# A gather of tokens for the experts, rebuilt with float32r one-hot slots and dealt out over the down products, with eight expert tiles loaded ahead

## The chip, the cores and the metric

One core of a Trainium2 chip runs the whole layer. The metric is device microseconds (us) for one execution. TensorE (PE) does the matrix products, VectorE (DVE), ScalarE (ACT) and GpSimd (POOL) the elementwise work, and DMA transfers are issued from the queues of SyncE (SP) and ACT.

## The reference, cut to what matters

The layer has two token mixers, a merge, an output projection and then a mixture of experts in which each of 16 experts chooses 64 of the 512 latent tokens. The part that the change touches is the expert stage:

```python
def expert_choice_ffn(h, router_w, w_gate, w_up, w_down):
    cap = max(1, (CAPACITY_FACTOR * n) // N_EXPERTS)          # 64
    aff = jax.nn.softmax(jnp.einsum('bnd,de->bne', h, router_w).astype(jnp.float32), axis=-1)
    gate, idx = lax.top_k(jnp.swapaxes(aff, 1, 2), cap)
    xs = jax.vmap(lambda hb, ib: hb[ib])(h, idx)              # the gather: 64 tokens of 2048 for each expert
    a = jnp.einsum('becd,edf->becf', xs, w_gate)
    u = jnp.einsum('becd,edf->becf', xs, w_up)
    y = jnp.einsum('becf,efd->becd', jax.nn.silu(a) * u, w_down) * gate[..., None].astype(h.dtype)
    ...                                                       # scatter-add back to the 512 tokens
```

Here h = modulate(rms_norm(x_lat)). The weights are float32: per expert 2048x1024 twice and 1024x2048 once, 24 MB, so 384 MB for the stage.

## The kernel before, in words

The program runs in this order: the input projections with the HGRN2 branch, then the gated DeltaNet branch, then `branches` (it reads the mixers' results, `yraw`, back on the ACT queue and splits them into a high and a low float32r part), `merge` (two branch products `pb0`, `pb1` for each of 16 blocks of channels), `project` (the output projection `po` and the router's logits `lg`), `prefetch` (which issues the first expert tiles), `route` (the top 64 of each expert) and `experts`.

Weights of the dense stages go through `split`: a 512 KB tile `wraw` (three buffers) is loaded on SP, ACT makes `whi` (two buffers), DVE makes `wlo`, and three products follow for each tile of weights. In `project` a step of 2 contraction blocks needs one `wraw` and feeds 24 products of 512 columns.

The experts are taken in pairs, two experts' 64 tokens making up the 128 rows. Each pair takes 48 tiles `ew` of 1 MB through `take()`: 32 of the gate and up weights, then 16 of the down weights. `pair(...)` takes two of them (one for each expert) and issues 8 products. `pgt`/`put` (tiles `pg`, `pu`) collect gate and up, `pys` (tiles `py`, `pu`) the down product. `prefetch` hands out the tiles: the first 18 (numbered 0 to 17 here) are issued ahead, 11 (`EW`) into the buffers `ew`, then 7 into `aa`, `row5`, four `xo` and `xs`, which are not used again for weights. From tile 18 on, tile n takes the buffer of the tile 11 before it in the ring of `ew`, once PE has used that one. Four of the 11 buffers (`ew1`) exist already while `project` runs, the other seven (`ew2`) only after it.

The gather before is one-hot: `begin` makes on DVE `oh`, a 128x64 one-hot tile for each of 4 token blocks and 2 experts, scaled by `rstd`, and on POOL `og`, the same scaled by the router's weight. `gather(pr, kc)` multiplies four blocks of channels of `x1` by it in plain float32 (16 products of 128 columns), and ACT applies the modulation to give `xs`. Two of a pair's four quarters run while the silu of the pair before is made, two after the products of k = 2 and k = 6 of the pair itself. After the last gate product `og` is transposed into `sct` and summed into `gs`. `scatter` puts the results back with `tokens`, dealt out by `step()` over the next pair's products.

PE's order in `branches` and in `experts` is the order of the code (a manual schedule); in `merge` and `project`, and on the other engines everywhere, a scheduler chooses it from a simulated timeline and from which memory is free. Each DMA also waits for the one that used its completion semaphore before; there are eight of these, dealt round over both queues.

Of the kernel before, what the change touches and what calls it, by code (L numbers as in the profile page):

```python
# [8 lines left out]
F32 = mybir.dt.float32  # L9
# [8 lines left out]
D = 2048  # L18
# [24 lines left out]
class Kern:  # L43
# [27 lines left out]
        return ap[:, k // 2 * 256 + k % 2:k // 2 * 256 + 256:2]  # L71

    pe = 0.0
    EW = 11
    pool_split = False

    def mm(self, out, lhsT, rhs, start=True, stop=True):
# [954 lines left out]
    def project(self):  # L1032
# [9 lines left out]
        self.bcol = self.fcol[:, 0]  # L1042
        V.tensor_scalar(self.acol, self.fcol[:, 1], 1.0, None, op0=OP.add)
        V.tensor_tensor(self.acol, self.acol, self.nffn, op=OP.mult)
        self.ew1 = self.pool("ew1", bufs=self.opt.get("e1", 4))
        sp = self.pool("pj")
        row2 = sp.tile([128, D], F32, name="row2")
        nc.scalar.dma_start(row2, self.row_d[0])
# [72 lines left out]
        self.close("pj")  # L1121
        self.close("m")
        self.close("w")
        self.ew2 = self.pool("ew2", bufs=self.EW - self.opt.get("e1", 4), side="right")

    def prefetch(self):

        nc, I = self.nc, self.I
        sp = self.ex = self.pool("ex")
        wg = I["w_gate"][0].rearrange("e (k p i) n -> e p k (i n)", p=128, i=2)  # L1130
        wu = I["w_up"][0].rearrange("e (k p i) n -> e p k (i n)", p=128, i=2)
        wd = I["w_down"][0].rearrange("e (k p) n -> e p k n", p=128)
        big = self.big = lambda: sp.tile([128, D], F32, name="xo", bufs=4)
        nld = [0]

        def load(t):
            src, pair = t
            n = nld[0]
            nld[0] += 1
            m = n - self.EW  # L1140
            if m in (0, 1):
                w = sp.tile([128, D], F32, name=("aa", "row5")[m])
            elif 2 <= m < 6:
                w = big()
            elif m == 6:
                w = sp.tile([128, D], F32, name="xs", bufs=2)
            else:
                if m > 6:
                    n -= 7
                w = (self.ew1 if n % self.EW < self.opt.get("e1", 4) else self.ew2).tile([128, D], F32, name="ew")  # L1150
            k, n = src.shape[1:]
            w = w[:, :k * n].rearrange("p (k n) -> p k n", k=k)
            nc.sync.dma_start(w, src)
            return w.rearrange("p k (i n) -> p (k i) n", i=2) if pair else w

        tiles = []
        for pr in range(E // 2):
            es = (2 * pr, 2 * pr + 1)
            for k in range(KT // 2):
                for w in (wg, wu):  # L1160
                    tiles += [(w[e][:, k:k + 1], True) for e in es]
            for ns in self.blocks(pr):
                n = self.rows(ns)
                for f in range(0, 8, n):
                    tiles += [(wd[e][:, f:f + n, ns], False) for e in es]
        ahead = [load(t) for t in tiles[:self.EW + 7]]
        rest = iter(tiles[self.EW + 7:])
        self.take = lambda: ahead.pop(0) if ahead else load(next(rest))

    def route(self):  # L1170
# [4 lines left out]
        xp = self.xp  # L1175
        self.slot = xp.tile([128, 4, 16], F32, name="slot")
        sp = self.ex
        t64 = lambda name, n: sp.tile([128, NL], F32, name=name, bufs=n)[:64, :256]
        pp = self.pool("rop", space=PSUM)
        A, wk, gt, eq, on, cs = (t64(n, b) for n, b in (("y", 2), ("y", 2), ("sct", 1), ("og", 1), ("oh", 2), ("oh", 2)))  # L1180
# [6 lines left out]
        m = xp.tile([64, 2, 64], F32, name="m64")  # L1187
        for i in range(8):
            src = wk if i else pa
            m8 = m[:, 0, i * 8:i * 8 + 8]  # L1190
# [44 lines left out]
    def experts(self):  # L1235
# [7 lines left out]

        def begin(pr):

            oh = sp.tile([128, 4, 2, 64], F32, name="oh", bufs=2)
            og = sp.tile([128, 4, 2, 64], F32, name="og", bufs=1)
            for t in range(4):
                for e in range(2):
                    n = 2 * pr + e  # L1250
                    V.tensor_scalar(oh[:, t, e], self.iota64, self.slot[:, t, n:n + 1], self.rstd[:, t:t + 1],
                                    op0=OP.is_equal, op1=OP.mult)
            for t in range(4):
                for e in range(2):
                    n = 2 * pr + e
                    G.tensor_scalar(og[:, t, e], self.iota64, self.slot[:, t, n:n + 1], self.rt[:, t % 2, t // 2 * 32 + n:t // 2 * 32 + n + 1],
                                    op0=OP.is_equal, op1=OP.mult)
            xs = sp.tile([128, D], F32, name="xs", bufs=2).rearrange("p (k n) -> p k n", k=KT)
            X[pr] = oh, og, xs

        def gather(pr, kc):
            oh, _, xs = X[pr][:3]
            px = pp.tile([128, 4, 128], F32, name="px")
            for j in range(4):
                k = kc * 4 + j
                for t in range(4):
                    self.mm(px[:, j], self.chan(x1[t], k), oh[:, t].rearrange("p e s -> p (e s)"),
                            start=(t == 0), stop=(t == 3))
            for j in range(4):
                k = kc * 4 + j  # L1270
                S.activation(xs[:, k], px[:, j], AF.Identity, scale=self.acol[:, k:k + 1], bias=self.bcol[:, k:k + 1])  # L1271

        def pair(outs, lhs, n, k0, m):

# [12 lines left out]
        def scatter(pr, pys, b, ns, act):  # L1287
            last = pr == E // 2 - 1
            items = []
            for u, py in enumerate(pys):  # L1290
                n = py.shape[1]
                cs = slice(ns.start + u * n, ns.start + u * n + n)
                if not last and u < 2:
                    y = act[:, u * 512:u * 512 + 512]
                else:
                    y = sp.tile([128, 512], F32, name="y", bufs=2)[:, :n]
                V.scalar_tensor_tensor(y, py, X[pr][4], row5[:, cs], op0=OP.mult, op1=OP.mult)
                items.append((y, cs, n, b + u))

            def parts(i):  # L1300

                y, cs, n, _ = items[i]
                yh = sp.tile([128, 512], F32R, name="yh", bufs=2)[:, :n]
                S.activation(yh, y, AF.Copy)
                yl = sp.tile([128, 512], F32R, name="yl", bufs=2)[:, :n]
                V.tensor_tensor(yl, y, yh.bitcast(F32), op=OP.subtract)
                items[i] += (yh, yl)

            def tokens(i, t):
                _, cs, n, b, yh, yl = items[i]  # L1310
                sct = X[pr][3][:, t * 128:t * 128 + 128]
                pz = pp.tile([128, 512], F32, name="px")
                self.mm(pz[:, :n], sct, yh, stop=False)
                self.mm(pz[:, :n], sct, yl, start=False)
                V.tensor_tensor(xo[t][:, cs], (x1 if pr == 0 else xo)[t][:, cs], pz[:, :n], op=OP.add)  # L1315
                if last:

                    S.activation(x1[t][:, cs], xo[t][:, cs], AF.Square, accum_out=ss[:, t, b:b + 1])
                    G.tensor_tensor(x1[t][:, cs], xo[t][:, cs], fn[:, cs], op=OP.mult)

            m = len(items)
            parts(0)
            if m > 1:
                parts(1)
            for i in range(m):
                for t in range(4):
                    todo.append((tokens, i, t))
                if i + 2 < m:
                    todo.append((parts, i + 2))
# [19 lines left out]
                S.activation(dst[:, b * 512:b * 512 + 512], pz, AF.Copy)  # L1349

        begin(0)
        gather(0, 0)
        gather(0, 1)
        for pr in range(E // 2):
            last = pr == E // 2 - 1
            oh, og, xs = X[pr][:3]
# [8 lines left out]
            for k in range(0, KT, 2):  # L1365
                pair(pgt, xs, KT, k, 2)
                step()
                pair(put, xs, KT, k, 2)
                step()
                if k in (2, 6):  # L1370
                    gather(pr, k // 4 + 2)
                if last and k == 8:
                    fn = sp.tile([128, D], F32, name="xs", bufs=2)
                    spread(fn, r)
            step(99)
            pg = pp.tile([128, 512], F32, name="px")
            for t in range(4):
                self.tr(pg[:, t * 128:t * 128 + 128], og[:, t].rearrange("p e s -> p (e s)"))

            gs = sp.tile([128, 1], F32, name="gs")  # L1380
            V.tensor_reduce(gs, pg, axis=AX.X, op=OP.add)
            sct = sp.tile([128, 512], F32R, name="sct")
            V.tensor_scalar(sct, pg, 0.0, None, op0=OP.is_gt)
            X[pr] += (sct, gs)
            for u in range(2):
                a = act[:, u * 512:u * 512 + 512]
# [2 lines left out]
                V.tensor_tensor(a, a, put[u], op=OP.mult)  # L1389
            if pr + 1 < E // 2:  # L1390
                begin(pr + 1)
                gather(pr + 1, 0)
                gather(pr + 1, 1)
            if pr == 0:
                row5 = sp.tile([128, D], F32, name="row5")
                spread(row5, r)
# [12 lines left out]
            for i, ns in enumerate(bl):  # L1409
# [4 lines left out]
                for f in range(0, 8, n):  # L1414
                    pair(pys, at, 8, f, n)
                    if last:
                        step(2)
                scatter(pr, pys, b, ns, act)
                b += len(pys)
        step(99)  # L1420
# [159 lines left out]
```

## Time and profile before

| | us |
|---|---|
| median of 3 runs | 3365.19 (3362.14 to 3375.09) |
| profiled execution | 3369.38 |
| its span | 3367.6 |
| PE busy | 3202.7 (95%) |
| DVE busy | 1446.2 (43%) |
| ACT busy | 871.8 (26%) |
| POOL busy | 395.0 (12%) |

Matmuls are pipelined and their ends are modelled, so a PE that is 95% busy is not at its peak: the starts of instructions tell more than their lengths. The span is cut into 40 slices on the page; in the last 11 of them, from about 2440 us, the DMA engines are busy 9 tenths and move about 420 GB/s, where they moved 57 to 305 GB/s before.

### The profile page before, as it was taken

How to read it: one execution, taken by the hardware profiler on the slowest of the kernel's cores; microseconds unless marked ns; L12 is line 12 of the kernel's file. 1: busy time of each engine (PE TensorE's matmuls, PEld its weight loads, DVE VectorE, ACT ScalarE, POOL GpSimd, SP SyncE). 2: the span in 40 equal slices, each digit the busy share in tenths (PEclk: the TensorE clock that was granted, in tenths of full speed). 3: DMA queues.
4: the chain of work that ended last, by engine and by line, in shares of the span. 5: the costliest groups of instructions: out<-in, count | busy, mean ns of one | idle time of the engine just before them, and what ended most of it. 6: DMA issues, size and time to landing. Idle time of an engine off the chain costs nothing.

```text
span 3367.6 us, 60040 instructions
## 1 busy us (share of the span) xinstructions
PE 3202.7 (95%) x25874; PEld 2316.7 (69%) x25874; DVE 1446.2 (43%) x2885; ACT 871.8 (26%) x1580; POOL 395.0 (12%) x327
## 2 busy tenths in 40 slices
PE   7999999999999969999999999999799999999997
PEld 5788888888788757777787878778444444444443
DVE  5325676676676653455555245332211111211113
ACT  4312322222223223444444332222111011010102
POOL 0000000000000113323222321000000000000002
PEclk8999999999999979999999999999899999999999
DMA  9934364564554444333232364621899999999998
GB/s 305 247 116 131 86 191 148 154 181 133 167 177 126 129 121 113 86 93 98 81 93 62 101 185 144 219 90 57 329 379 420 420 420 420 420 420 421 420 421 302
DMA packets 454057, 726.01 MB, mean 216 GB/s; under 512 B 21531, under 2 KB 330995, under 8 KB 404767
## 3 DMA queue, kind: packets, MB, share of 16 engines
q1 hardware_dynamic: 425263, 674.75, 57.2%
q10 hardware_dynamic: 28528, 47.43, 4.0%
q8 instruction: 203, 3.33, 0.4%
q14 instruction: 63, 0.52, 0.0%
HBM read 690.57 MB, written 31.53 MB: 214 GB/s over the span
## 4 chain that ended last, share of the span: by engine, by line
PE 46%; DVE 3%; DMA 2%; ACT 1%; issue 1%; ACTq 0%; SPq 0%; DVEq 0%
PE pu L80 12%; PE pg L80 7%; PE px L80 6%; PE pb L80 5%; PE po L80 5%; PE pl L80 5%; PE mx L80 2%; PE py L80 2%; DMA wraw<-in_w_out 1%; DMA ew<-in_w_gate 0%; DMA yraw<-y_d 0%; DMA gm<-G_d 0%; PE lg L80 0%; ACT xs L1271 0%; PE pt L85 0%
## 5 line engine op out<-in xcount | busy, mean ns | idle before, releaser
L80 PE MATMUL pl<-hlh,whi 128*128 128x512 f32 (+1 forms) x1552 | 633.5, 408 | 0.7 <-ACT vo L323 0.7
L80 PE MATMUL pl<-hll,whi 128*128 128x512 f32 (+1 forms) x1552 | 614.6, 396 | 0.0
L80 PE MATMUL pl<-hlh,wlo 128*128 128x512 f32 x1536 | 610.3, 397 | 2.9 <-DVE wlo L341 2.8
L339 ACT ACTIVATE whi<-wraw 128x1024 fp32r<-128x1024 f32 (+1 forms) x280 | 289.6, 1035 | 907.2 <-PE pl L80 224.7
L341 DVE TENSOR_TENSOR wlo<-wraw,whi 128x1024 fp32r<-128x1024 f32 (+1 forms) x200 | 258.0, 1290 | 282.2 <-ACT whi L339 282.1
L80 PEld LDWEIGHTS pl<-hlh,whi 128*128 128x128 f32 (+1 forms) x1552 | 293.9, 189 | 59.4 <-ACT vo L323 1.1
L80 PEld LDWEIGHTS pl<-hlh,wlo 128*128 128x128 f32 x1536 | 291.8, 190 | 48.2 <-DVE wlo L341 4.5
L80 PEld LDWEIGHTS pl<-hll,whi 128*128 128x128 f32 (+1 forms) x1552 | 294.2, 190 | 37.2 <-issue 0.7
L341 POOL TENSOR_TENSOR wlo<-wraw,whi 128x1024 fp32r<-128x1024 f32 x80 | 192.6, 2407 | 475.6 <-ACT whi L339 421.1
L80 PE MATMUL pg<-ew,xs 128*64 128x512 f32 x992 | 247.9, 604 | 0.5 <-DMA ew<-in_w_gate 0.5
L967 DVE SCALAR_TENSOR_TENSOR aacc<-awt,sc,aacc 128x512 f32<-128x512 f32 x256 | 209.6, 819 | 82.7 <-DMA awt<-in_ada_w 73.8
L80 PE MATMUL pu<-ew,xs 128*64 128x512 f32 x1000 | 243.2, 600 | 0.0
L1315 DVE TENSOR_TENSOR xo<-xo,px 128x512 f32<-128x512 f32 (+1 forms) x116 | 76.8, 668 | 360.7 <-PE px L80 360.7
L80 PE MATMUL py<-ew,aa 128*64 128x512 f32 (+1 forms) x608 | 230.8, 584 | 0.0
L80 PE MATMUL pu<-ew,aa 128*64 128x512 f32 x448 | 199.5, 592 | 0.0
L80 PEld LDWEIGHTS pu<-ew,xs 128*64 128x64 f32 x1000 | 89.9, 136 | 122.7 <-issue 115.3
L80 PEld LDWEIGHTS pg<-ew,xs 128*64 128x64 f32 x992 | 84.5, 137 | 122.9 <-issue 114.4
L80 PE MATMUL pcx<-hch,whi 128*128 128x256 f32 (+1 forms) x528 | 150.0, 284 | 0.0
L80 PE MATMUL pcx<-hcl,whi 128*128 128x256 f32 (+1 forms) x528 | 149.1, 282 | 0.0
L80 PE MATMUL pcx<-hch,wlo 128*128 128x256 f32 x512 | 146.0, 285 | 0.0
L80 PEld LDWEIGHTS pu<-ew,aa 128*64 128x64 f32 x448 | 61.6, 137 | 119.0 <-issue 119.0
L80 PEld LDWEIGHTS px<-oh,x 128*128 128x128 f32 x1024 | 125.9, 199 | 7.9 <-DVE xo L1315 4.0
(455 smaller groups left out, 4852.5 us busy)
## 6 DMA issues: line engine op xcount, KB each, us to landing
ew<-in_w_up SPq DMA_DIRECT2D x125, 1024.0 KB
ew<-in_w_gate SPq DMA_DIRECT2D x124, 1024.0 KB
ew<-in_w_down SPq DMA_DIRECT2D x124, 1024.0 KB
wraw<-in_w_in SPq DMA_DIRECT2D x208, 512.0 KB
awt<-in_ada_w SPq DMA_DIRECT2D x128, 512.0 KB
aw<-in_ada_w SPq DMA_DIRECT2D x32, 1024.0 KB
wraw<-in_w_out SPq DMA_DIRECT2D x24, 512.0 KB
mg_d<-mg ACTq DMA_DIRECT2D x32, 256.0 KB
```

The costliest lines, as they stand in the source:

```text
L80: self.nc.tensor.matmul(out, lhsT, rhs, start=start, stop=stop, skip_group_check=True)
L339: nc.scalar.activation(hi[:, :n], raw[:, :n], AF.Copy)
L341: eng.tensor_tensor(lo[:, :n], raw[:, :n], hi[:, :n].bitcast(F32), op=OP.subtract)
L967: V.scalar_tensor_tensor(acc, w[:, k], self.sc[:, k0 + k, 0:1], acc, op0=OP.mult, op1=OP.add)
L1315: V.tensor_tensor(xo[t][:, cs], (x1 if pr == 0 else xo)[t][:, cs], pz[:, :n], op=OP.add)
```

## The change

The gather is turned round. `begin` makes `oh` as plain 0/1 in float32r, and it is now the stationary operand. `gparts` makes, for a block of 256 channels, the high part `gh` (ACT, scaled by `rstd`) and the low part `gl` (DVE) of `x1`, both float32r; 8 products of 256 columns give the 128 gathered rows, DVE copies them out (`gy`), two transposes turn them into the layout of `xs`, and ACT modulates as before. `gather` is now a generator of 16 pieces (8 blocks, a products piece and a transposes piece of each). For pair 0 three pieces run first and the rest after each gate and up product; for every later pair the pieces run after the down products of the pair before, one after the first of its eight and two after each other one, and the last piece after the next pair's first gate product. `og` goes; `gs` comes from 4 small products of `oh` and the router's weights `rt`. `EW` is 12 and `e1` is 8: eight buffers of the ring exist while `project` runs, 19 tiles are issued ahead. The scratch for descriptors at the start of each SBUF partition is 1 KB, which makes room for the buffers.

```diff
-    EW = 11
+    EW = 12
...
-        self.ew1 = self.pool("ew1", bufs=self.opt.get("e1", 4))
+        self.ew1 = self.pool("ew1", bufs=self.opt.get("e1", 8))
...
-        self.ew2 = self.pool("ew2", bufs=self.EW - self.opt.get("e1", 4), side="right")
+        self.ew2 = self.pool("ew2", bufs=self.EW - self.opt.get("e1", 8), side="right")
...
-                    V.tensor_scalar(oh[:, t, e], self.iota64, self.slot[:, t, n:n + 1], self.rstd[:, t:t + 1],
-                                    op0=OP.is_equal, op1=OP.mult)
...
-                    G.tensor_scalar(og[:, t, e], self.iota64, self.slot[:, t, n:n + 1], self.rt[:, t % 2, t // 2 * 32 + n:t // 2 * 32 + n + 1],
-                                    op0=OP.is_equal, op1=OP.mult)
+                    V.tensor_scalar(oh[:, t, e], self.iota64, self.slot[:, t, n:n + 1], None, op0=OP.is_equal)
...
+        def gparts():
+            for b in range(8):
+                cs = slice(b * 256, b * 256 + 256)
+                h = sp.tile([128, 4, 256], F32R, name="gh")
+                l = sp.tile([128, 4, 256], F32R, name="gl")
                 for t in range(4):
-                    self.mm(px[:, j], self.chan(x1[t], k), oh[:, t].rearrange("p e s -> p (e s)"),
-                            start=(t == 0), stop=(t == 3))
+                    S.activation(h[:, t], x1[t][:, cs], AF.Copy, scale=self.rstd[:, t:t + 1])
+                    V.scalar_tensor_tensor(l[:, t], x1[t][:, cs], self.rstd[:, t:t + 1], h[:, t].bitcast(F32),
+                                           op0=OP.mult, op1=OP.subtract)
+                yield h, l
+
+        def gather(pr):
+            oh, xs = X[pr][:2]
+            parts = gparts()
+            p = next(parts)
+            for b in range(8):
+                px = pp.tile([128, 512], F32, name="px")
+                for t in range(4):
+                    for a in p:
+                        self.mm(px[:, :256], oh[:, t], a[:, t], start=(t == 0 and a is p[0]),
+                                stop=(t == 3 and a is p[1]))
+                y = sp.tile([128, 256], F32, name="gy")
+                V.tensor_copy(y, px[:, :256])
+                p = next(parts, None)
+                yield
+                px = pp.tile([128, 2, 128], F32, name="px")
+                for i in range(2):
+                    self.tr(px[:, i], y[:, i::2])
...
+                yield
...
-        gather(0, 0)
-        gather(0, 1)
+        ga = gather(0)
+        for _ in range(3):
+            next(ga)
...
                 pair(pgt, xs, KT, k, 2)
                 step()
+                next(ga, None)
                 pair(put, xs, KT, k, 2)
                 step()
-                if k in (2, 6):
-                    gather(pr, k // 4 + 2)
+                next(ga, None)
...
+                self.mm(pg[:, 0:2], ohf[:, t], self.rt[:, t % 2, t // 2 * 32 + 2 * pr:t // 2 * 32 + 2 * pr + 2],
+                        start=(t == 0), stop=(t == 3))
...
                 begin(pr + 1)
-                gather(pr + 1, 0)
-                gather(pr + 1, 1)
+                ga = gather(pr + 1)
...
                     if last:
                         step(2)
+                    else:
+                        next(ga, None)
+                        if f:
+                            next(ga, None)
...
-    nc = bacc.Bacc("TRN2", target_bir_lowering=False, num_devices=1)
+    nc = bacc.Bacc("TRN2", target_bir_lowering=False, num_devices=1, dynamic_dma_scratch_size=1024)
```

On SP's queue, at the start of `project` (`wraw<-in_w_out` are its weights, `ew` the early expert tiles):

```order
-L338 DMA wraw<-in_w_out 128x2x512 x4
-L1153 DMA ew<-in_w_gate 128x2048 x2
-L1153 DMA ew<-in_w_up 128x2048
-L338 DMA wraw<-in_w_out 128x2x512
-L1153 DMA ew<-in_w_up 128x2048
+L338 DMA wraw<-in_w_out 128x2x512 x5
+L1153 DMA ew<-in_w_gate 128x2048 x2
+L1153 DMA ew<-in_w_up 128x2048 x2
+L1153 DMA ew<-in_w_gate 128x2048 x2
+L1153 DMA ew<-in_w_up 128x2048 x2
 L338 DMA wraw<-in_w_out 128x2x512 x19
```

The fifth tile of the projection's weights moved ahead of the expert tiles, and eight expert tiles, not four, stand ahead of the sixth.

On ACT, at the end of `branches` (`yraw` are the mixers' results read back, `yh` their high parts; `row_21640` is the projection's 1 MB row `row2`, `rw` the router's weights), a piece of before:

```order
L1013 DMA g_20585<-mg_d_102 128x512
L993 DMA yraw<-y_d_58 128x512
L994 ACTIVATE yh_20295<-yraw 128x512
L993 DMA yraw<-y_d_58 128x512 x2
L339 ACTIVATE whi<-wraw 128x1024
```

and the same place now:

```order
L1013 DMA g_20585<-mg_d_102 128x512
L1048 DMA row_21640<-row_d_125 128x2048
L993 DMA yraw<-y_d_58 128x512
L994 ACTIVATE yh_20295<-yraw 128x512
L993 DMA yraw<-y_d_58 128x512
L1052 DMA rw<-in_router_w 128x8x32
L993 DMA yraw<-y_d_58 128x512
```

The loads of `row2` and `rw` moved here from the start of `project`, where they stood on ACT after the four loads of `x1`; the small products that use `rw` (`pt`, 16 of them) moved on PE from within the projection to its start.

On PE, from the last gate and up products of pair 0 to its first down products (`og` the weighted one-hot, `x_0` to `x_3` the four token blocks of `x1`), before, up to the first four of the 32 products of the gather:

```order
L80 MATMUL pg<-ew,xs 64x512 x8
L80 MATMUL pu<-ew,xs 64x512 x8
L85 MATMUL px<-ident,og 128x128 x4
L80 MATMUL px<-oh,x_0_21625 128x128
L80 MATMUL px<-oh,x_1_21626 128x128
L80 MATMUL px<-oh,x_2_21627 128x128
L80 MATMUL px<-oh,x_3_21628 128x128
```

and now (`rt` the router's weights, `y` the row that is spread over 128 partitions, `aa` the silu's result):

```order
L80 MATMUL pg<-ew,xs 64x512 x8
L80 MATMUL pu<-ew,xs 64x512 x8
L85 MATMUL px<-ident,oh 128x128 x4
L80 MATMUL px<-rt,oh 128x2 x4
L80 MATMUL px<-y,ident 128x512 x4
L85 MATMUL px<-ident,aa 128x128 x8
L80 MATMUL py<-ew,aa 64x512 x2
```

The 32 products of the gather between silu and down products are gone from here; the pieces of the new gather stand behind each pair of down products.

## Rows read from the trace of the kernel before

**Rows 1.** Windows: us, then busy time (count) of each engine, PEclk, DMA share, GB/s.
```profile
2395.00:2400.00 5.00, 5.00 (x26) 2.13 (x24) 0.00 (x0) 0.25 (x1) 0.00 (x0) 1.00 0.59 197
...
2430.00:2435.00 5.00, 5.00 (x26) 1.99 (x24) 1.42 (x7) 2.34 (x5) 0.00 (x0) 1.00 0.00 0
...
2475.00:2480.00 5.00, 5.00 (x15) 1.61 (x15) 0.00 (x0) 0.00 (x0) 0.00 (x0) 0.74 0.01 3
...
2600.00:2700.00 100.00, 100.00 (x455) 42.70 (x452) 19.31 (x35) 6.62 (x14) 0.00 (x0) 1.00 1.01 421
...
3335.00:3340.00 5.00, 5.00 (x37) 2.90 (x37) 3.40 (x6) 2.92 (x8) 2.99 (x3) 1.00 0.90 294
```

**Rows 2.** SP's own instructions in order of time: start us, us, what, count.
```profile
2153.35 0.81 SPq L1153 DMA_DIRECT2D ew<-in_w_gate  x2
...
2397.32 0.80 SPq L1153 DMA_DIRECT2D ew<-in_w_up  x2
2400.75 0.80 SPq L1153 DMA_DIRECT2D ew<-in_w_gate  x2
...
2418.65 18.23 SPq L1153 DMA_DIRECT2D ew<-in_w_gate  x2
...
2440.40 46.33 SPq L1153 DMA_DIRECT2D ew<-in_w_down  x16
```

**Rows 3.** The chain that ended last, in order of time: start us, us, what.
```profile
2991.81 4.31 PE pg L80 x16
2996.78 4.33 PE pu L80 x16
...
3289.52 3.63 PE pg L80 x16
3293.82 3.63 PE pu L80 x16
...
3302.41 3.68 PE pu L80 x16
...
3309.92 10.45 PE py L80 x48
...
3344.21 1.90 PE py L80 x16
```

**Rows 4.** PE's instructions in order of time, pair 0: start us, us, what [idle before].
```profile
2383.57 10.14 PE L80 MATMUL px<-oh,x 128*128 128x128 f32 x64 [0.99 <-DVE oh L1251]
...
2457.60 7.70 PE L80 MATMUL px<-oh,x 128*128 128x128 f32 x64
...
2473.79 3.68 PE L80 MATMUL py<-ew,aa 128*64 128x512 f32 x4
```

**Rows 5.** A window of the projection; ACT and DVE instructions with 128x256 operands.
```profile
2350.00:2355.00 5.00, 5.00 (x44) 5.00 (x43) 1.13 (x2) 1.26 (x2) 0.00 (x0) 1.00 0.00 0
...
2360.28 0.42 ACT L1086 ACTIVATE jk<-x 128x256 f32<-128x256 f32 x1
...
2359.29 0.75 DVE L1085 TENSOR_TENSOR x<-x,y 128x256 f32<-128x256 f32 x2
```

**Rows 6.** The chain at the projection's start; DVE's first result of it.
```profile
2156.60 21.72 DMA wraw<-in_w_out
...
2185.64 3.48 PE pt L80 x32
2189.12 19.15 PE po L80 x84
...
2203.54 1.37 DVE L1084 TENSOR_TENSOR y<-po,row 128x512 f32<-128x512 f32 x2 [1.08 <-PE po L80]
```

**Rows 7.** The chain at the end of the branches; PE's first products of the merge.
```profile
1957.08 6.22 DMA yraw<-y_d
...
1971.58 0.50 PE L80 MATMUL pb<-yh,whi 128*128 128x512 f32 x1 [2.83 <-ACT mg L950]
...
1972.78 0.63 PE L80 MATMUL pb<-yl,whi 128*128 128x512 f32 x1
```

More of the change, by code (lines that the diff above doesn't have):

```diff
@@ L1149, in load @@
                     n -= 7
-                w = (self.ew1 if n % self.EW < self.opt.get("e1", 4) else self.ew2).tile([128, D], F32, name="ew")
+                w = (self.ew1 if n % self.EW < self.opt.get("e1", 8) else self.ew2).tile([128, D], F32, name="ew")
             k, n = src.shape[1:]
@@ L1177, in route @@
         sp = self.ex
-        t64 = lambda name, n: sp.tile([128, NL], F32, name=name, bufs=n)[:64, :256]
+        t64 = lambda name, n: sp.tile([128, 1024 if name == "gh" else NL], F32, name=name, bufs=n)[:64, :256]
         pp = self.pool("rop", space=PSUM)
-        A, wk, gt, eq, on, cs = (t64(n, b) for n, b in (("y", 2), ("y", 2), ("sct", 1), ("og", 1), ("oh", 2), ("oh", 2)))
+        A, wk, gt, eq, on, cs = (t64(n, b) for n, b in (("y", 2), ("y", 2), ("sct", 1), ("gh", 1), ("oh", 2), ("oh", 2)))
         G.memset(on, 1.0)
@@ L1185, in route @@
         S.activation(A, pa, AF.Copy)
-        m = xp.tile([64, 2, 64], F32, name="m64")
+        m = sp.tile([128, NL], F32, name="yh", bufs=2)[:64, :128].rearrange("p (a b) -> p a b", a=2)
         for i in range(8):
@@ L1244, in begin @@
         def begin(pr):
-            oh = sp.tile([128, 4, 2, 64], F32, name="oh", bufs=2)
-            og = sp.tile([128, 4, 2, 64], F32, name="og", bufs=1)
+            oh = sp.tile([128, 4, 2, 64], F32R, name="oh", bufs=2)
             for t in range(4):
@@ L1250, in begin @@
                     n = 2 * pr + e
-                    V.tensor_scalar(oh[:, t, e], self.iota64, self.slot[:, t, n:n + 1], self.rstd[:, t:t + 1],
-                                    op0=OP.is_equal, op1=OP.mult)
-            for t in range(4):
-                for e in range(2):
-                    n = 2 * pr + e
-                    G.tensor_scalar(og[:, t, e], self.iota64, self.slot[:, t, n:n + 1], self.rt[:, t % 2, t // 2 * 32 + n:t // 2 * 32 + n + 1],
-                                    op0=OP.is_equal, op1=OP.mult)
@@ L1258, in begin @@
-            xs = sp.tile([128, D], F32, name="xs", bufs=2).rearrange("p (k n) -> p k n", k=KT)
[L1259 to L1265, printed above, removed]
-                for t in range(4):
-                    self.mm(px[:, j], self.chan(x1[t], k), oh[:, t].rearrange("p e s -> p (e s)"),
-                            start=(t == 0), stop=(t == 3))
-            for j in range(4):
-                k = kc * 4 + j
-                S.activation(xs[:, k], px[:, j], AF.Identity, scale=self.acol[:, k:k + 1], bias=self.bcol[:, k:k + 1])
+                    V.tensor_scalar(oh[:, t, e], self.iota64, self.slot[:, t, n:n + 1], None, op0=OP.is_equal)
@@ new lines, in begin @@
+            xs = sp.tile([128, D], F32, name="xs", bufs=2).rearrange("p (k n) -> p k n", k=KT)
+            X[pr] = oh.rearrange("p t e s -> p t (e s)"), xs
+        def gparts():
[3 more added lines that the diff above has]
+                l = sp.tile([128, 4, 256], F32R, name="gl")
+                for t in range(4):
+                    S.activation(h[:, t], x1[t][:, cs], AF.Copy, scale=self.rstd[:, t:t + 1])
+                    V.scalar_tensor_tensor(l[:, t], x1[t][:, cs], self.rstd[:, t:t + 1], h[:, t].bitcast(F32),
+                                           op0=OP.mult, op1=OP.subtract)
+                yield h, l
@@ new lines, in gather @@
+        def gather(pr):
[15 more added lines that the diff above has]
+                    self.tr(px[:, i], y[:, i::2])
+                for i in range(2):
+                    k = 2 * b + i
+                    S.activation(xs[:, k], px[:, i], AF.Identity, scale=self.acol[:, k:k + 1],
+                                 bias=self.bcol[:, k:k + 1])
+                yield
@@ L1296, in scatter @@
                     y = sp.tile([128, 512], F32, name="y", bufs=2)[:, :n]
-                V.scalar_tensor_tensor(y, py, X[pr][4], row5[:, cs], op0=OP.mult, op1=OP.mult)
+                V.scalar_tensor_tensor(y, py, X[pr][3], row5[:, cs], op0=OP.mult, op1=OP.mult)
                 items.append((y, cs, n, b + u))
@@ L1310, in tokens @@
                 _, cs, n, b, yh, yl = items[i]
-                sct = X[pr][3][:, t * 128:t * 128 + 128]
+                sct = X[pr][2][:, t * 128:t * 128 + 128]
                 pz = pp.tile([128, 512], F32, name="px")
@@ L1351, in experts @@
         begin(0)
-        gather(0, 0)
-        gather(0, 1)
+        ga = gather(0)
+        for _ in range(3):
+            next(ga)
         for pr in range(E // 2):
             last = pr == E // 2 - 1
-            oh, og, xs = X[pr][:3]
+            oh, xs = X[pr][:2]
             aa = sp.tile([128, D], F32, name="aa")
@@ L1375, in experts @@
             step(99)
+            for _ in ga:
+                pass
+            ohf = oh.bitcast(F32)
             pg = pp.tile([128, 512], F32, name="px")
             for t in range(4):
-                self.tr(pg[:, t * 128:t * 128 + 128], og[:, t].rearrange("p e s -> p (e s)"))
+                self.tr(pg[:, t * 128:t * 128 + 128], ohf[:, t])
+            sct = sp.tile([128, 512], F32R, name="sct")
+            V.tensor_copy(sct, pg)
+            pg = pp.tile([128, 512], F32, name="px")
+            for t in range(4):
+                self.mm(pg[:, 0:2], ohf[:, t], self.rt[:, t % 2, t // 2 * 32 + 2 * pr:t // 2 * 32 + 2 * pr + 2],
+                        start=(t == 0), stop=(t == 3))
             gs = sp.tile([128, 1], F32, name="gs")
-            V.tensor_reduce(gs, pg, axis=AX.X, op=OP.add)
-            sct = sp.tile([128, 512], F32R, name="sct")
-            V.tensor_scalar(sct, pg, 0.0, None, op0=OP.is_gt)
+            for e in range(2):
+                V.tensor_copy(gs[e * 64:e * 64 + 64], pg[e * 64:e * 64 + 64, e:e + 1])
             X[pr] += (sct, gs)
```

## The prediction, on record before the changed kernel ran

> **What bounds the kernel now.** I read the page's slices first, then windows over the expert stage, then the chain in order of time, then SP's queue and PE at the places that the change touches. The slices say that the last quarter is one stream of weights; a window inside it shows a DMA share of 1.01 and 421 GB/s [rows 1], that is 1.0486 MB / 0.4205 = 2.49 us for a tile of 1 MB. Pair 0 alone is different. Its 18 tiles are there before PE starts, PE takes two tiles each 3.43 us (the distance of SP's issues at 2397.32 and 2400.75, which wait for PE to give buffers back) [rows 2], and a tile can be loaded only when the one 11 places earlier in the ring has been used. So the stream stands still three times: about 2 us before 2397 (share 0.59 in five us), some 11 us around 2432 (share 0.00; the buffers of tiles 11 to 17 are not given back, and SP waits inside its row at 2418.65 for tile 18 to be used), and some 7 us around 2477 (share 0.01), while PE is between silu and the first down products [rows 1, 2]. It starts again near 2480, within SP's row of 16 down tiles, with tile 43, which takes the buffer of tile 32, and then runs to the end: 384 - 43 = 341 tiles behind 2480. **The time of that last restart and the number of tiles behind it set the end of the kernel.** In the middle of a later pair products start 4.97 us apart, which is two tiles of DMA (2991.81 and 2996.78); in the last pair they start 4.30 us apart (3289.52 and 3293.82), which is PE's own pace with the scatter, and the end, from 3302.41 to 3346.1, is PE's chain and not the stream's, whose last bytes land at about 3339.5 [rows 1, 3].
>
> **The gather, pair 0.** Before, PE's first gather starts at 2383.57 and takes 10.14 us, partly at half clock, then the products follow [rows 4]. After, the same moment has 8 products of 256 columns. 44 such products of the projection take 5.00 us, 0.114 us each [rows 5], so a block is 0.91 us at full clock, 1.8 at half. Then DVE copies (0.38), PE transposes, and before the second block's products ACT and DVE must make the next parts: four of 0.42 us on ACT, DVE one step behind (0.75 / 2 = 0.38) [rows 5], 2.4 us with the hand-overs. 1.9 + 2.4 + 1.8 makes the first gate product about 2390, 3.6 us earlier; but PE has then done less, and I charge 2 us for products at half clock. Net 1.6. The 16 steps of 3.43 us are unchanged; between them lie 6 more blocks (5.5 us) and 14 transposes (about 2 us) instead of two gathers of 3.9 (half of 7.70), no difference.
>
> **The pause of pair 0.** Before, 2457.1 to 2473.79: 7.70 us of it is the gather for pair 1 [rows 4], 9.0 us are transposes, the spreading of a row over 128 partitions, and waits. The gather goes from here. What is late next is the silu: its sigmoid can run under the last up product, its last two products on DVE and the copy that frees a PSUM buffer for the spreading cannot. I take 8 us, with 1 us back from a shorter pause's clock. So the first down products stand at about 2463 and the buffer of tile 32 comes free 11 us earlier, plus the 1.6: the stream restarts near 2467.5, 12.5 us earlier. With 12 buffers and 19 tiles ahead it restarts with tile 44: one tile, 2.5 us, less behind it. **Together -15.** Bounds: if the pause shrinks by nothing, 1.6 + 2.5 remain, about -4. If it shrinks more, the stop before it decides: tile 31 waits for tile 19, ten steps and half the gather after 2392, 2433 with the start of a transfer; 13 tiles at 2.49 are 32.4, so 2465.4 at the earliest, and -17.
>
> **The gather, pairs 1 to 7.** Per pair 31 us of ACT and DVE work come in (32 parts of 0.42 and 0.38, 16 results), hidden on engines that are busy 7 and 19 us of 100 [rows 1]. PE: 64 products (7.3) and 16 transposes (2.3) for 15.6 before. A down step is 3.43 + 0.91 + 0.25 = 4.6 us, below the stream's 4.97; the round products, parts, products is 0.91 + 2.4 + 0.3 = 3.6 us, below the step. So the stream stays the bound there: nothing. At the end, two quarters of the gather (7.8 us) leave the last pair's gate and up products; PE keeps up, and the end is the last landing plus one product group of 1.9 us and what follows, 3341.4 + the rest, where PE's last group ended at 3346.1 [rows 1, 3]: -4.5 at most, 0 at least if the spreading in that pair still makes it late; I take **-3.5**.
>
> **The loads at the start of the projection.** The first four expert tiles no longer come before the fifth weight tile, and eight come before the sixth. Before, the fifth, issued at 2156.60, landed 21.72 us later, behind three expert tiles and beside `x1` [rows 6]. After, what must land up to the sixth is 4.2 MB of `x1`, 0.5, 8.4 and 0.5: 13.6 MB, 32.4 us at 0.4205, from about 2155.4 on (the first expert tile was issued at 2153.35 [rows 2]): 2187.8, and about 1 us for the split. PE has the small `pt` products (3.48) and five steps of 24 products at 0.228 (19.15 / 84) [rows 6], 27.4 us, from 2153.35: idle from 2184.2 to 2188.9. Three more steps end at 2205.3, where the first result before came at 2203.54: +1.8, and I add 2 us for half clock after a stop of nearly 5: **+4**. Bounds: -3 if the sixth tile comes in time (2184.2 and three steps are 2200.6), +10 if the rate falls as it does beside loads with short rows.
> The Trainium skill (DMA: Bandwidth & Descriptors, Queues, rings and completion order) speaks against the change here: each DMA engine takes its rings' descriptors in order and goes round between rings, so a small load behind eight large ones waits for all of them. By that rule the term is the +4; were the sixth tile let past, it would be the -3. The row of 21.72 us for half a megabyte agrees with the rule.
>
> **The loads moved to the branches' end.** `row2` and `rw`, 1.18 MB, now go out on ACT's queue among the `yraw` loads, one of which took 6.22 us, and PE waited 2.83 us there, after which products took 0.63 us for the usual 0.39 or 0.40 [rows 7]. At 0.42 MB per us they delay the chain by 2.8 us: **+3**, bounds 0 (two fewer results are now asked for before PSUM comes free) and +6, one more such load.
>
> **Sum.** -15 - 3.5 + 4 + 3 = -11.5: 3369.38 - 11.5 = 3357.9 for the profiled execution, which lies 4.2 us above the runs' median of 3365.19. On that scale **3354**.
>
> **Rivals.**
> - *The gain is taken back before the experts.* The projection waits +10, the branches +6, the pause saves half: +16 - 9.5 - 3.5 = +3, 3368. For it: both places wait already [rows 6, 7]. Against: the bytes give only half of that.
> - *More than forecast.* Restart at the earliest (-17), the tail's -4.5, projection 0, branches 0: -21.5, 3344. For it: the scheduler put both moves where its timeline saw memory and time. Against: 8.4 MB ahead of one 0.5 MB tile.
> - *Slower: the round through three engines sets the down steps.* Each block waits for ACT and DVE, with one buffer for the parts. A pair has 119.7 us of stream; gate and up products with scatter take 16 x 4.30 = 69, the pause 5, which leaves 46 for eight steps: from 5.7 us a step on PE is the bound. At 7 us it costs 8 x 1.3 x 7 = 73 us, 3427. Against: 3.6 us from the rows [rows 5]; half as much again would still be hidden.
> - *Slower: PE falls to half clock.* With less to do PE waits more on each tile, and pairs no longer have a gather in the pause. At 1.2 GHz a step is 6.86 us, above 4.97: 24 x 1.9 = 45 us a pair, 3400 if only one pair runs so. Against: the granted clock is 1.00 in the stream [rows 1], with waits of 0.67 us a step already. The Trainium skill (TensorE: Matmul & The Clock Gate, HAM oscillation — how this bites in real kernels) tells of kernels that wait for DMA between short bursts of products and run at half clock for it; no row of this stream shows it.
> - *The early loads do nothing:* they would only move bytes if the stream's restart did not depend on the tiles ahead. Then -12.5 for the pause stays and 2.5 is lost, 3356, inside the forecast's own range.
>
> **How the numbers follow.** Forecast 0.63, with 3343 to 3365 as its own range; taken back 0.15; more 0.14; the round 0.04; the clock 0.04. A measurement of this kernel can tell about 0.5%, 16.8 us: below 3348.4 lie most of "more" and a fifth of the forecast, 0.28; above 3382 the two slow rivals, 0.08; the rest, 0.64, is within. The range 3340 to 3369 holds the forecast, most of "taken back" and most of "more".
>
> **What would show it.** Right: one stop of the stream near 2470 of 3 us or less, none after; products in the down steps about 5 us apart; PE idle some 5 us near 2185; the last products within 3 us of the last landing. Wrong: down steps above 5.7 us, PEclk below 1.00 after 2500, a stop of the stream in a later pair, or a projection that waits 10 us and more.

## The result and the profile after

| | before | after |
|---|---|---|
| median | 3366.46 us (4 runs, 3362.14 to 3375.09) | 3425.39 us (4 runs, 3417.84 to 3429.42) |
| profiled execution, its span | 3369.38, 3367.6 | 3426.09, 3424.2 |

The ratio is 1.0169 (95%: 1.0142 to 1.0196): slower, where I forecast 3354 and at most 3369. The starts of the products `pg` (first gate product of a pair) and `py` (first down product) in the two profiles say where it went; each row is the difference of two such starts.

| stretch | before | after | difference |
|---|---|---|---|
| to pair 0's first `pg` | 2393.64 | 2394.72 | +1.1 |
| pair 0, first `pg` to first `py` | 80.15 | 80.14 | 0.0 |
| pair 0, first `py` to pair 1's first `pg` | 30.22 | 54.77 | +24.6 |
| pairs 1 to 6, first `pg` to the last pair's first `pg` | 717.08 | 757.48 | +40.4 |
| last pair, first `pg` to its last product | 123.05 | 113.70 | -9.4 |
| from there to the end | 23.46 | 23.39 | -0.1 |

That is +56.6, the whole difference of the spans. Both profiles are single executions, and ahead of the experts executions differ: in the profiles of all kernels here the first `pg` lies between 2389.64 and 2405.83. The +65.0 of pairs 0 to 6 is far beyond that, and it arises in the down steps. Windows of the kernel after, with the columns of [rows 1]:

```profile
2395.00:2400.00 5.00, 5.00 (x16) 1.36 (x14) 1.83 (x5) 1.31 (x4) 0.00 (x0) 0.64 0.02 8
...
2435.00:2440.00 5.00, 5.00 (x24) 1.81 (x21) 0.00 (x0) 0.81 (x2) 0.00 (x0) 1.00 0.00 0
...
2475.00:2480.00 5.00, 5.00 (x14) 1.67 (x15) 0.00 (x0) 0.56 (x1) 0.00 (x0) 0.79 0.31 125
...
2600.00:2700.00 100.00, 99.94 (x410) 41.35 (x412) 31.05 (x69) 23.48 (x54) 0.00 (x0) 1.00 0.98 392
```

All three stops of the stream are still there, and in the middle of the stage it moves 392 GB/s where it moved 421 [rows 1]: PE is busy for 99.94 of 100 us at full clock, and the stream waits for PE. A stretch of the chain of the kernel after, in order of time (start us, us, what), from pair 1's last up products to pair 2's first gate products:

```profile
2594.37 3.68 PE pu L80 x16
...
2602.20 1.93 PE py L80 x4
...
2607.62 1.14 PE px L80 x8
2608.76 1.86 PE py L80 x4
...
2615.50 1.86 PE py L80 x4
...
2622.24 1.86 PE py L80 x4
...
2655.94 3.64 PE pg L80 x16
```

Down steps start 6.74 us apart, all on PE, in every pair but the last. Sixteen gate and up steps and the pause take 72.6 us, the eight down steps 53.7, together 126.25 us a pair, where before it was 117.6 to 120.6. PE's own instructions in one such step, in order of time (start us, us, operands, tile sizes, count, and in brackets idle time before, of which there is none):

```profile
2615.43 1.93 PE L80 MATMUL py<-ew,aa 128*64 128x512 f32 x4
2617.20 0.59 PE L80 MATMUL pu<-ew,aa 128*64 128x512 f32 x1
2617.21 0.64 PE L80 MATMUL py<-ew,aa 128*64 128x512 f32 x1
2617.63 0.59 PE L80 MATMUL pu<-ew,aa 128*64 128x512 f32 x1
2617.69 0.59 PE L80 MATMUL py<-ew,aa 128*64 128x512 f32 x1
...
2618.97 1.88 PE L80 MATMUL pu<-ew,aa 128*64 128x512 f32 x4
2620.79 0.50 PE L85 MATMUL px<-ident,gy 128*128 128x128 f32 x2
2621.05 0.36 PE L80 MATMUL px<-gh,oh 128*128 128x256 f32 x1
...
2621.96 0.28 PE L80 MATMUL px<-gl,oh 128*128 128x256 f32 x1
2622.17 1.07 PE L80 MATMUL py<-ew,aa 128*64 128x512 f32 x2
```

The eight products of a step (two records each) multiply by 64 columns: expert 0's results go to partitions 0 to 63, expert 1's to 64 to 127, and `pair` issues expert 0's four first (`py`, `py`, `pu`, `pu`), then expert 1's four. The array takes two of them at once only when they belong to different experts: four records run alone (1.8 us), eight run in pairs (a `pu` and a `py` start 0.01 us apart), four run alone (1.8 us). In a row of steps without anything between, one step's lonely end lies beside the next step's lonely beginning, so a step costs 3.43 us. A product of 128 columns between the steps cuts that, and the step costs 2620.79 - 2615.43 = 5.36 us, and 1.38 for the pieces.

The Trainium skill (TensorEngine Tiling (Array Packing), Key Properties) says that changing the tiling mode, not just the tile, drains TensorE. The rows agree that a 128-column product waits for the 64-column ones: the last four `pu` records start at 2618.97 and take 1.88 us, and the transposition starts at 2620.79. The Trainium skill (TensorE: Matmul & The Clock Gate, Part 3: Packing small matmuls — row/col tiling) says that products start strictly in program order. The rows differ: a `py` that can only be expert 1's, since expert 0's four records of `py` are done, starts at 2617.21, ahead of expert 0's last `pu`.

The round through the three engines is not what binds. Grouped by shape (busy us, mean ns, idle us just before them and what ended it), over all 64 blocks:

```profile
L80 PE MATMUL px<-gh,oh 128*128 128x256 f32 x256 | 70.8, 309 | 1.6 <-DVE oh L1250 1.6
...
L85 PE MATMUL px<-ident,gy 128*128 128x128 f32 x128 | 31.7, 330 | 0.5 <-DVE gy L1278 0.5
```

PE waited 1.6 us for one-hot tiles and 0.5 us for a copy in the whole run, and for parts never.

### The profile page after: what moved, and what is told of

Its sections match the earlier page's. It is cut to its first block, busy times and chain, and to the rows that moved or that the text cites. A ratio compares the mean times of both kernels' runs of the same rounds, so it can differ in the third digit from the quotient of the medians.

```text
span 3424.2 us, 59978 instructions
## 1 busy us (share of the span) xinstructions
PE 3259.6 (95%) x25554; PEld 2280.6 (67%) x25554; DVE 1572.8 (46%) x3213; ACT 982.3 (29%) x1836; POOL 357.5 (10%) x263
## 3 DMA queue, kind: packets, MB, share of 16 engines
q1 hardware_dynamic: 425263, 674.75, 56.6%
## 4 chain that ended last, share of the span: by engine, by line
PE 48%; DVE 3%; DMA 2%; ACT 1%; issue 0%; ACTq 0%; DVEq 0%; SPq 0%
PE pu L80 12%; PE pg L80 7%; PE pb L80 5%; PE pl L80 5%; PE po L80 5%; PE px L80 5%; PE py L80 4%; PE mx L80 2%; PE px L85 1%; DMA wraw<-in_w_out 1%; PE lg L80 0%; DMA ew<-in_w_gate 0%; DMA gm<-G_d 0%; DMA yraw<-y_d 0%; PE pt L85 0%
## 5 line engine op out<-in xcount | busy, mean ns | idle before, releaser
L80 PE MATMUL py<-ew,aa 128*64 128x512 f32 (+1 forms) x608 | 239.2, 587 | 0.3
L80 PE MATMUL pu<-ew,xs 128*64 128x512 f32 x1000 | 233.3, 601 | 0.0
L80 PE MATMUL pg<-ew,xs 128*64 128x512 f32 x992 | 233.1, 609 | 0.0
L1278 DVE COPY gy<-px 128x256 f32<-128x256 f32 x64 | 27.2, 425 | 292.7 <-PE px L80 292.7
L80 PEld LDWEIGHTS pg<-ew,xs 128*64 128x64 f32 x992 | 77.0, 138 | 122.1 <-issue 117.1
L80 PEld LDWEIGHTS pu<-ew,xs 128*64 128x64 f32 x1000 | 77.1, 136 | 118.9 <-issue 115.6
```

The costliest lines, as they stand in the source:

```text
L80: self.nc.tensor.matmul(out, lhsT, rhs, start=start, stop=stop, skip_group_check=True)
L1278: V.tensor_copy(y, px[:, :256])
```

## The experiments

Three theories stood against each other: the cut between the two halves of the array (A), the round with one buffer for the parts (B), the early loads (C). Ratios are to the kernel before, on the same chip.

**1. Alternate the experts** (kernel after):

```diff
-                for i in range(2):
-                    r = slice(i * 64, i * 64 + 64)
-                    for u, o in enumerate(outs):
+                iu = [(i, u) for i in range(2) for u in range(len(outs))]
+                if m == 1:
+                    iu.sort(key=lambda x: x[1])
+                for i, u in iu:
```

> The changed kernel with one edit: in a down step the eight products alternate between the two experts (expert 0 block 0, expert 1 block 0, ...) instead of four of one expert and then four of the other. Everything else, the gather's pieces and the round over ACT and DVE included, stays. Theory A (the two 64-column halves of the array work side by side only while products of both experts are next in line; a 128-column piece between two steps leaves each half alone for two products at either end, 5.36 us instead of 3.43): a down step falls from 6.74 to about 3.43 + 0.2 + 1.38 = 5.0 us, a pair needs 16 x 4.30 + 3.5 + 8 x 5.0 = 112 us of PE, below the 119.9 of the stream, so the seven pairs give back about 7 x 6.3 = 44 us: 3381 or, since the stream then restarts as early as before and with one buffer more, down to 3364. Theory B (the round products, copy, transposes, parts with one buffer each sets the step, PE waits in it): the step stays near 6.7 us and the time at 3425, within 4 us. Theory C (the early loads): 3425 as well.

Measured: 3371.89 us, before 3375.03, ratio 0.999 (0.9975 to 1.0005). PE's instructions in a down step, and a window, of this kernel:

```profile
2609.97 1.94 PE L80 MATMUL py<-ew,aa 128*64 128x512 f32 x8
2611.73 1.89 PE L80 MATMUL pu<-ew,aa 128*64 128x512 f32 x8
2613.55 0.51 PE L85 MATMUL px<-ident,gy 128*128 128x128 f32 x2
2613.82 0.36 PE L80 MATMUL px<-gh,oh 128*128 128x256 f32 x1
...
2614.94 1.94 PE L80 MATMUL py<-ew,aa 128*64 128x512 f32 x8
```
```profile
2600.00:2700.00 100.00, 100.00 (x453) 41.23 (x452) 31.40 (x62) 22.77 (x53) 0.00 (x0) 1.00 1.01 420
```

Eight records of `py` now take the time that four took; the step is 4.97 us, the first full pair 112.1, and from pair 3 on the stream sets 119.8 to 120.5 again. With the round unchanged, B falls; A is shown.

**2. The kernel before, and one transposition behind each down step:**

```diff
+                    else:
+                        pz = pp.tile([128, 512], F32, name="px")
+                        self.tr(pz[:, :128], self.ident)
```

> The kernel before with one edit: after each down step of pairs 0 to 6 one transposition of the constant identity, 128x128, into a free PSUM tile that nobody reads. No gather moves, no parts, no round over ACT and DVE, the old loads. Theory A (the interruption itself costs): a down step becomes 5.36 + 0.3 = 5.6 to 5.7 us instead of 3.43; the pair's PE work goes from about 117 to 134 us, above the stream's 119.9, so +14 us a pair in seven pairs: 3440 to 3465. Theory B or C (an interruption costs its own 0.3 us, what hurt was the round or the loads): 8 x 0.3 = 2.4 us a pair, hidden under the stream: 3366 to 3372.

Measured: 3461.67 us, ratio 1.0268 (1.0249 to 1.0288). PE in one step:

```profile
2640.36 0.33 PE L85 MATMUL px<-ident 128*128 128x128 f32 x1
2640.62 1.93 PE L80 MATMUL py<-ew,aa 128*64 128x512 f32 x4
...
2644.16 1.88 PE L80 MATMUL pu<-ew,aa 128*64 128x512 f32 x4
2645.97 0.33 PE L85 MATMUL px<-ident 128*128 128x128 f32 x1
```

A step of 5.61 us from a transposition that occupies 0.26: 5.35 are the products. The pairs follow at 132.5 us; 134 was expected. It is the cut, without any gather in it.

**3 and 4. Gather and loads apart.** Run 3 is the kernel after with `EW = 11` and `e1` 4; run 4 the kernel before with `EW = 12`, `e1` 8 and the scratch of 1 KB.

> The changed kernel with the old ring: 11 buffers, 4 of them ahead of the projection. The new gather stays. Theory A or B (the down steps set the pairs): steps of 6.74 us and pairs of 126.25 us as in the changed kernel; only what the early loads cost ahead of the experts comes back, about 3 us: 3418 to 3425. Theory C (the twelve buffers and the eight early tiles are what costs): near 3366.

> The kernel before with the new ring alone: 12 buffers, 8 of them ahead of the projection, descriptor scratch of 1 KB. The old gather stays. Theory A or B: pairs of 119.9 us as in the kernel before; +3 to +6 us ahead of the experts, -2.5 us for one tile less behind the restart: 3366 to 3370. Theory C: 3410 or more.

Measured: 3419.74, ratio 1.0143 (1.0123 to 1.0163); and 3374.24, ratio 1.0005 (0.9995 to 1.0015). The kernel before took 3375.03 us beside these runs, so it is the ratios that can be set against the times expected. The slowdown goes with the gather; the loads cost or bring nothing that can be told. C falls.

**5 to 8. From the repaired kernel on, one edit after the other.** Run 5 is run 1 with `e1` 4. Run 6 adds the first edit below, run 7 the second; run 8 alternates in the gate and up steps too.

```diff
-            if pr == 0:
-                r = row(self.row_d[1][0])
...
+                if pr == 0 and k == 8:
+                    row5 = sp.tile([128, D], F32, name="row5")
+                    nc.scalar.dma_start(row5, self.row_d[1][0:1].to_broadcast([128, D]))
...
-            if pr == 0:
-                row5 = sp.tile([128, D], F32, name="row5")
-                spread(row5, r)
```
```diff
                 step()
                 next(ga, None)
+                next(ga, None)
                 pair(put, xs, KT, k, 2)
                 step()
-                next(ga, None)
```

> The changed kernel with the alternating order of the first experiment, and 4 instead of 8 expert tiles ahead of the projection (12 buffers stay). If the eight early tiles only cost (the sixth weight tile waits behind them) and the ring is full by the time PE reaches the experts either way, the projection gets its 3 to 4 us back and nothing else moves: 3 to 4 us below the first experiment, 6 to 7 us below the kernel before (ratio 0.998). If the early tiles are needed for the ring to be full in time, no gain or a loss of 2 to 3 us against the first experiment (ratio 0.999 to 1.000).

> As the run before it in this list, and the row of 2048 numbers that PE spreads over 128 partitions in pair 0's pause (four products, 6.69 us there) is loaded by one DMA of 1 MB, spread by the descriptors, onto the same tile in the middle of pair 0's gate and up steps, where the stream stands still for 11 us. If PE's pause in pair 0 sets the stream's restart, and that the end: the pause falls from 10.6 to 4 us, the restart comes 6.5 us earlier and the end with it: 13 us below the kernel before (ratio 0.996). If something else bounds the restart or the end (the last pair is PE's own chain), 0 to 3 us of it is seen (ratio 0.997 to 0.998). If the load lands late, the first scatter waits and it is slower than the run before it.

> As the run before it, and in the gate and up steps of pair 0 the transposes and the next block's products stand together behind each gate step instead of one behind the gate and one behind the up step: six or seven interruptions fewer. Theory A (an interruption of the paired products costs some 0.2 us at a gate or up step, and 0.2 more at the piece): 2 to 3 us earlier restart, 15 to 16 us below the kernel before (ratio 0.995). Against it: the transposes then stand right behind 3.63 us of products with the copy long done, so no wait is added; a wait on the parts (2.1 us of ACT and DVE) has 7.3 us of cover. No change if the number of interruptions does not matter there.

> As the run before it, with the products alternating between the experts in the gate and up steps as well (two products of each expert in a row there now). Theory A: a gate or up step with an interruption after it takes 3.63 us, one without 3.43; with two products of each in a row only 0.2 us are lost, so alternating can bring 0 to 0.2 us a step, in pair 0 at most 16 x 0.2 = 3 us and nothing in the pairs that the stream sets: 15 to 19 us below the kernel before (ratio 0.994 to 0.9955).

| run | median us (before 3373.26) | ratio |
|---|---|---|
| 5 | 3363.01 | 0.9970 (0.9960 to 0.9980) |
| 6 | 3361.84 | 0.9961 (0.9947 to 0.9975) |
| 7 | 3357.78 | 0.9954 (0.9942 to 0.9966) |
| 8 | 3358.87 | 0.9958 (0.9946 to 0.9970) |

In run 5 PE's longest wait at the projection's start is 2.35 us, where the kernel after has 4.56. The steps between neighbours lie inside their intervals; from 1 to 7 the sum is clear. Run 6 was expected 6.5 us below run 5, and the medians show 1.2. The profiled executions show where the rest is. Two stretches of each (us between starts, and to the end of the span):

| | before | after | run 1 | run 5 | run 6 | run 7 | run 9 | run 11 |
|---|---|---|---|---|---|---|---|---|
| pair 0, first `pg` to first `py` | 80.15 | 80.14 | 77.32 | 77.46 | 71.03 | 70.53 | 73.85 | 68.68 |
| from there to the end | 893.8 | 949.3 | 890.9 | 892.4 | 893.0 | 892.0 | 889.7 | 892.2 |

Run 6 has the 6.4 us inside pair 0, and except in the kernel after the end comes 890 to 894 us behind the first `py` in all of them. What varies is the time ahead of the experts: the six executions of run 6 lie between 3351.36 and 3372.70 us, and in the profiled one the first `pg` stands at 2405.83, in run 5's at 2392.78. Run 7 and run 11 are the same kernel; in run 7 the first gate step took 5.55 us instead of 3.71, at a granted clock of 0.58 in 2390 to 2395. Without that, the pieces standing together bring 2.35 us (71.03 to 68.68), of 2 to 3 expected.

The chain of run 7 around pair 0's pause, and two of its windows:

```profile
2454.19 3.43 PE pu L80 x16
2457.62 0.60 PE px L85 x4
...
2460.93 1.94 PE py L80 x8
```
```profile
2430.00:2440.00 10.00, 10.00 (x54) 5.09 (x55) 2.45 (x6) 3.77 (x10) 0.00 (x0) 1.00 0.67 229
...
3320.00:3330.00 10.00, 10.00 (x72) 5.88 (x72) 6.33 (x12) 5.45 (x17) 7.45 (x6) 1.00 0.55 180
```

The pause is 3.3 us (10.6 in the kernel after), the stream stops once after 2400, near 2435 and for 3 us, and its last bytes land in that second window; in the kernel before they did at about 3339.5. Run 8 brings nothing: its uncut gate steps are 3.43 us as before, its cut ones 3.58 instead of 3.63.

**9 to 11. What the moved gather is worth, and the last spread.** Run 9 is the kernel before with the ring of 12 (`e1` 4, scratch 1 KB) and the row by DMA; run 10 is run 7 with the last pair's row loaded like pair 0's; run 11 is run 7 again.

> The kernel before, gather as it was, with the ring of 12 buffers (4 early, scratch of 1 KB) and the spread of pair 0's row by one DMA. What it tells: how much of the gain of the pieces-together run comes from the moved gather. If the pause of pair 0 alone sets the restart, the gather for pair 1 (7.70 us) still stands in it: the pause falls by the spread's 6.5 us and one tile (2.5 us) less lies behind the restart, 6 to 9 us below the kernel before (ratio 0.997 to 0.998), and the pieces-together kernel stays 6 to 9 us ahead of it. If the moved gather brings nothing, the two are equal within 3 us.

> The pieces-together kernel with the second spread too, that of the last pair's row (four products of PE and four copies of ACT in its gate steps), replaced by one DMA of 1 MB. If PE's chain in the last pair sets the end (steps 4.30 us apart, the last products 5 us behind the last bytes), the end comes up to 3.5 us earlier: ratio 0.994 to 0.9955. If the stream's 1 MB more cancels it, no change or 2.5 us later.

> The pieces-together kernel once more, unchanged, so that the two runs beside it are compared on one chip: ratio 0.9942 to 0.9966 as measured before, if the chip makes no difference.

Measured, with 3371.97 for the kernel before: 3365.62, ratio 0.9976 (0.9966 to 0.9987); 3359.08, 0.9954 (0.9940 to 0.9967); 3359.06, 0.9955 (0.9941 to 0.9970). PE of run 9, pair 0's pause:

```profile
2468.45 7.70 PE L80 MATMUL px<-oh,x 128*128 128x128 f32 x64
...
2478.33 1.93 PE L80 MATMUL py<-ew,aa 128*64 128x512 f32 x4
```

The old gather still stands there with its 7.70 us, and the medians of runs 9 and 11 are 6.6 us apart, within the expected 6 to 9; their intervals overlap by 0.0004. In the profiles 5.2 us of it lie inside pair 0 (73.85 and 68.68 in the table above). The last row's DMA brings nothing.

## Why the prediction was wrong

**The step that failed** is "A down step is 3.43 + 0.91 + 0.25 = 4.6 us, below the stream's 4.97 ... So the stream stays the bound there: nothing". The step is 6.74. Of the missing 2.15 us, 1.93 is the products themselves (5.36 for 3.43, the cut, shown by runs 1 and 2) and 0.22 the pieces (1.38 for 1.16). I took 3.43 as the price of eight products, but it was their spacing in an unbroken row. The prediction's own sign of being wrong, down steps above 5.7 us, came. The profile before already held the warning: its first `py` row [rows 4] is a group of four records alone, in front of which a transposition stands. It also held the cure. In the last pair the down product is made in narrow blocks, and there `pair` issues the products of the two experts in turn; full-width products of the scatter stand between these steps, and eight products still take 3334.45 - 3330.87 = 3.58 us (kernel before, PE's instructions):

```profile
3330.87 3.65 PE L80 MATMUL py<-ew,aa 128*64 128x512 f32 x16
3334.45 0.51 PE L80 MATMUL px<-yh,sct 128*128 128x512 f32 x1
```

Eight steps at 3.31 us more (1.93 and 1.38) are 26.5 us a pair. In pair 0 nearly all of it is seen, the +24.6 of the table; in pairs 1 to 6 the old gather's time goes off and the stream covers a part, and 126.25 us a pair against the 119.5 of before is the +40.4.

**The rival that gave 3427** had the right time for the wrong reason: it bounded the step at 5.7 us rightly and took 7, but named waits on ACT and DVE. PE had none for the parts, and run 1 took 1.8 us out of the step with the round unchanged. Its chance of 0.04 followed from judging only that mechanism.

**Pair 0's pause, -15 forecast.** First `py` at 2463 was forecast, 2474.86 came. The forecast itself does not add up to 2463: 2457.1 + 8 - 1 is 2464.1, and if the gather's 1.6 is already in the 2463, "plus the 1.6" counts it twice; that is 1 to 2 us of the term. A part of the kernel after's chain:

```profile
2394.78 5.52 PE pg L80 x16
...
2448.65 1.15 PE px L80 x8
2449.80 3.63 PE pg L80 x16
2453.43 0.44 PE px L85 x2
2453.87 3.63 PE pu L80 x16
2457.50 3.44 PE pg L80 x16
2460.94 3.43 PE pu L80 x16
...
2466.33 6.69 PE px L80 x8
...
2474.93 2.96 PE py L80 x4
```

A gate or up step with a piece behind it takes 3.63, one without 3.43, and the pieces 1.15 and 0.44: a round of two steps 8.85, 2.0 above two bare steps. Six such rounds and one more transposition are 12.5 us, where I had 7.5 and set it against the gather's 7.7. The first step takes 5.52, at a granted clock of 0.64 in 2395 to 2400. The pause itself fell from 16.7 to 10.6, 8 was forecast: the spread of the row (6.69) stands in it as before, at a granted clock of 0.50 in 2470 to 2475. So pair 0 gained nothing in this execution; in run 1, where its gate and up steps are the same and the first of them was not slowed, it gained 2.8 us. The mechanism was right, the size was not: with the spread gone and fewer cuts (runs 6, 7 and 11) the first `py` follows the first `pg` up to 11.5 us sooner than in the kernel before, and the end keeps its distance to it.

**The projection, +4:** right, also in its working. Its rows after, of the chain and of PE and DVE (answering to [rows 6]):

```profile
2171.14 20.19 DMA wraw<-in_w_out
...
2192.54 21.54 PE po L80 x84
```
```profile
2192.54 2.08 PE L80 MATMUL po<-whi,mh 128*128 128x512 f32 x4 [4.56 <-ACT whi L339]
...
2209.35 1.37 DVE L1084 TENSOR_TENSOR y<-po,row 128x512 f32<-128x512 f32 x2 [1.08 <-PE po L80]
```

An idle time of 4.56 where 4.7 was forecast, and the first result 5.8 us later, 4.2 of it here if the 1.6 of the branches stands in the rest. **The branches, +3:** +1.6 (PE's first `pb` at 1973.17 for 1971.58 [rows 7]). **The gather ahead of pair 0, -1.6:** 3.6 was forecast up to the first gate product and 2 charged for the clock behind it. The first part gained 5.1, since the gather's first product is 6.2 us later and the first `pg` only 1.1; the first step then took 1.9 more than before, so the net is 3.2. All three are read from one execution of each kernel. **The tail, -3.5:** the last pair takes 9.4 us less. Two quarters of the gather have left it (7.7 us: two rows of 32 products, 3.85 each), and its first steps no longer wait for weights (4.97 us apart before, about 4.3 now), which comes of starting 66 us late. In run 1, where the stream sets the pairs again, the last pair takes 119.4 us for 123.05: -3.7, as forecast.

**Clock and chances.** PEclk (the granted clock as a share of the full one) is 1.00 in every window of 100 us from 2500 to 3300 of the kernel after, so that rival did not come. 0.08 on slower was too little for a change that puts 128-column work into every down step of pairs 0 to 6, rows that nothing had broken in the trace.

## What to carry to other kernels

The time of one step in an unbroken row of small-tile products is not the price of that step: before putting anything between two steps, look at how the first and last products of a row lie in the trace, and count what no longer overlaps. Alternate the products of the two halves of the array, so that each neighbour can run beside the one before it; then a cut cost 0.2 us here instead of 1.9. Work moved off a pause still counts where it lands when PE is the bound there, as in pair 0.

## What was not expected of the hardware

A transposition of 0.26 us behind each of 56 down steps made the kernel 87 us slower (run 2, medians). Four products in a row for one half of the array delay the other half by two products (1.8 us), two in a row by next to nothing (3.63 us for a step instead of 3.58 when alternated). Why the second half starts at the third product and not at the first is not settled by these runs.
